# Where the tiles of a decoder trunk begin in SBUF: 160 and 288 bytes past a multiple of 512, or at it

## The chip, the cores and the metric

The kernel runs on one core of a Trainium2 chip. The metric is the time of one execution on the device, in microseconds (us); lower is better. Three executions of the kernel before took 2289.76, 2294.25 and 2301.1 us; the median is 2294.25 us.

## The reference, cut to what matters

Two decoder layers work on 256 tokens of width 2048, all in float32. Each is a mixer with an input and an output projection, and then a dense SwiGLU feed-forward part of width 5632.

```
h = x
for layer in range(2):
    p = rms_norm(h, norm[layer]) @ w_in[layer]
    # layer 0: a gated convolution and RWKV-7;  layer 1: a pooling mixer and latent attention
    h = h + mixer(p) @ w_out[layer]
    xf = rms_norm(h, ffn_norm[layer])
    h = h + (silu(xf @ w_gate[layer]) * (xf @ w_up[layer])) @ w_down[layer]
return rms_norm(h, final_norm)
```

All but a small part of the arithmetic is in the dense products `@ w`.

## The kernel before, in words

**A float32 product from three passes.** Each activation x and each weight w is split into a rounded float32r part (hi) and the rest (lo). A product is then xh·wh + xl·wh + xh·wl, so each 128 rows of the contraction cost three matmuls. A matmul has a stationary operand of 128 columns, which a weight load (PEld in the profile) brings into TensorE, and a moving operand of 256 or 512 columns, which is streamed past it. Every matmul of the dense products changes the stationary operand, so there is one weight load for each matmul, and the load for the next one runs while the present one streams.

**Two forms of the dense product.** `gemm_wt` (L160) takes 128 columns of weights (`wh`, `wl`) as stationary and 256 tokens of `xh` or `xl` as moving: the input projections. `gemm_tok` (L173) takes 128 tokens of `xh` or `xl` as stationary and 512 columns of weights as moving: the output projections and the gate and up products. The down products use `gemm_tok` with `hh` and `hl`, the split hidden activations, as stationary; the keys, queries and values of the odd layer use `lh` and `ll`, the split latents.

**The weights' path.** SP issues a DMA for each half block (`load_next`, L67: `w`, 1024 columns, 512 KB). ScalarE rounds 512 columns of it to `wh` (L96) and VectorE subtracts to give `wl` (L97); `quarter` (L106) hands them to the matmuls. There are 4 buffers of `w` and 6 each of `wh` and `wl`. The instructions' order on each engine is the order of the program's text; nothing is reordered later.

**Where tiles lie.** `build` (L286) opens pools one behind the other, and a pool's tiles lie in the order in which their tags are first asked for. The constants are first, from byte 16,512 of each partition: `ident`, `ones`, `pkt`, `mhalf`, `cos`, `sin` and `h`, which ends at byte 37,024. The pool `xs` follows: `xh` and `xl` (4 buffers of 4096 bytes each), then `dg` (2 x 512 bytes), `ssq` and `rstd` (2 x 32 each), which are asked for later. Then comes the pool `wp`: `w`, `wh`, `wl`; and then the pools of the stages. All buffers of the tags in the table are a multiple of 2048 bytes long, and slices of 128 columns are 512 bytes, so what a tile's start leaves over a multiple of 512 also holds for each operand sliced from it:

| operand | start of the first buffer | over a multiple of 512 |
|---|---|---|
| `xh`, `xl` | 37,024 | 160 |
| `w` | 70,944 | 288 |
| `wh`, `wl` | 87,328 | 288 |
| `hh`, `hl` (feed-forward stages) | 120,096 | 288 |
| `lh`, `ll` (odd layer's latents) | 117,088 | 352 |

Of the kernel before, what the change touches and what calls it, by code (L numbers as in the profile page):

```python
# [10 lines left out]
F32 = mybir.dt.float32  # L11
# [7 lines left out]
P = 128  # L19
T = 256  # L20
# [31 lines left out]
class Trunk:  # L52
# [12 lines left out]

# [1 line left out]
    def load_next(self):  # L67
        """the next half of a block; its split into parts frees the space of the fourth after it"""
        if not self.blocks:
            return  # L70
        src = self.blocks[0]
        w = self.wp.tile([P, 1024], F32, tag="w", name="w", bufs=WBUFS)
        o = self.half * 1024
        if isinstance(src, list):
            for i in range(2):
                self.nc.sync.dma_start(
                    out=w[:, i * 512 : i * 512 + 512], in_=src[2 * self.half + i]
                )
            end = self.half
        else:  # L80
            self.nc.sync.dma_start(out=w, in_=src[:, o : o + 1024])
            end = o + 1024 == src.shape[-1]
        self.loaded.append((w, 0))
        self.half = 0 if end else 1
        if end:
            self.blocks.pop(0)
# [19 lines left out]
    def quarter(self):  # L106
        """the next 512 columns of weights; what waits in the background moves on"""
        self.fill()
        self.tick()
        return self.pend.pop(0)  # L110

# [1 line left out]
    def later(self, n, fn):  # L113
# [22 lines left out]
    def drain(self, gen=None):  # L136
        """emits the background's steps up to the end of gen"""
        while self.lane and (gen is None or any(g is gen for g in self.lane)):
            self.step()
# [6 lines left out]
    def split(self, dst, src, scale=None):  # L146
        """dst (hi, lo) float32r <- src [* scale per partition]"""
        nc = self.nc
        hi, lo = dst
        if scale is None:  # L150
            nc.scalar.activation(hi, src, AF.Copy)  # L151
            nc.vector.tensor_tensor(out=lo, in0=src, in1=hi.bitcast(F32), op=ALU.subtract)  # L152
        else:
            nc.scalar.activation(hi, src, AF.Copy, scale=scale)
            nc.vector.scalar_tensor_tensor(
                out=lo, in0=src, scalar=scale, in1=hi.bitcast(F32),
                op0=ALU.mult, op1=ALU.subtract,
            )

    def gemm_wt(self, X, n=4, tag="mm"):  # L160
        """[128 columns of W, tok] = W^T X over n quarters of 4 k tiles"""
        out = self.ps(tag)[:, :T]
# [10 lines left out]
    def gemm_tok(self, X, kcs, out=None, stop=True):  # L173
        """out [tok, 512] x 2 halves (+)= X W over the k tiles 4 kc .. 4 kc + 3 of each kc"""
        new = out is None
# [13 lines left out]

# [1 line left out]
    def transpose_nb(self, X, gname, nb):  # L191
        """512 columns of h (token-major) -> x^T parts, with the norm's gain folded in"""
        nc = self.nc
# [38 lines left out]
    def finish(self, ps, nb, ssq, X, gname):  # L232
        """adds a layer's last part to 512 columns of h and turns them into x^T parts"""
        self.add_h(ps, nb, ssq)
        self.later(3, lambda: self.transpose_nb(X, gname, nb))

    def out_proj(self, M, n0, before, gname):
        """h += M W: all but the last blocks ahead of the last heads; before(kc) makes M[kc]"""
        pool = self.xs
# [11 lines left out]
        X = self.xtiles()  # L251
# [4 lines left out]

# [1 line left out]
    def order(self):  # L258
# [27 lines left out]
    def build(self):  # L286
# [4 lines left out]
        with (  # L291
# [11 lines left out]
            self.sin = cp.tile([P, T], F32, name="sin")  # L303
            self.h = cp.tile([P, 2, D], F32, name="h")
            nc.vector.memset(self.mhalf, -0.5)
            nc.vector.memset(self.ones, 1.0)
# [14 lines left out]
    def last(self, HX, kcs, ssq):  # L321
        """the last 512 columns and the final norm, one half of the tokens ahead of the other"""
        nc, a, V = self.nc, self.a, self.nc.vector
# [49 lines left out]
    def sums_tok(self, out, xs, w):  # L373
        """out [tok, ...] = sum of x^T w for both halves of the tokens; x [128, 256]"""
        n = w.shape[-1]
# [7 lines left out]
    def rsqrt(self, out, ps, scale, eps):  # L383
        """out = (scale ps + eps) ** -0.5"""
        n = out.shape[-1]
# [5 lines left out]
    def row_bcast(self, rb, rs):  # L391
        """rb [128, 256] <- rs [tok, 2], each token's value on every partition"""
        nc = self.nc
# [6 lines left out]

# [1 line left out]
    def ffn(self, X, ssq, gname, between=None):  # L402
# [60 lines left out]

# [1 line left out]
    def even_mix(self):  # L465
# [6 lines left out]

        # x^T parts, by pieces that alternate with the first weights
        X = self.xtiles()
# [9 lines left out]
        gmask, blk, smask = cst[:, 0:128], cst[:, 128:256], cst[:, 256:516]  # L484
        # 1/rms, as a row on every partition
        rb = tp.tile([P, T], F32, name="rb0")
# [19 lines left out]

        # space of h until x is loaded there
        hv0, hv1 = self.h[:, 0], self.h[:, 1]
# [41 lines left out]
        def first_tiles():  # L550
            """four column tiles at once, so that x^T is wanted no faster than it comes"""
            warm = self.ps()
# [59 lines left out]
        def spread(out, v):  # L612
            """out [128, tok] <- v [tok, (half, head)], each head on its 64 partitions"""
            vx = ta("vx").rearrange("p (t h n) -> p t h n", t=2, h=2)
# [12 lines left out]
        def open_group(grp):  # L627
            """even heads on partitions 0-63 with rows (B | K), odd heads on 64-127 with (K | B)"""
            g = {}
# [12 lines left out]
        def prep_a(ti):  # L642
            """decays and key norms of two heads"""
            i = ti % 4
# [33 lines left out]
            S.activation(ch(Ei), cum[:, :, 1:65], AF.Exp, scale=KAPPA)  # L678
            # 1 / norm of the keys, [tok, half, head]
            kn = tp.tile([P, 4], F32, tag="kn", name="kn", bufs=2)  # L680
# [7 lines left out]
        def prep_b(ti):  # L688
            """keys, values and the Gram matrices of two heads"""
            grp, i = ti // 4, ti % 4  # L690
# [6 lines left out]
            for w in range(4):  # L697
                nc.tensor.transpose(  # L698
                    pv[:, w * P : w * P + P], v[:, w * 64 : w * 64 + P], self.ident
                )  # L700
            # window w has chunk w on rows 0-63 and chunk w + 1 on 64-127
            pvv = pv.rearrange("p (w h n) -> p w h n", w=4, h=2)
# [41 lines left out]
            S.activation(BKt[:, i], pb.rearrange("p (c n) -> p c n", c=4), AF.Copy)  # L744
            # Gram matrices, rows at s, columns (Z | R) at t
            for hh in range(2):
# [11 lines left out]
                )  # L758
                # N goes to TT, its 32 x 32 diagonal blocks also to DG; its place in G takes Z
                for q in range(2):  # L760
# [12 lines left out]
        def recur(grp):  # L773
            """the recurrence over four chunks of 64 tokens, eight heads at a time"""
            g = groups[grp]
            g2, G, TT, UV, BKt, bv = (g[n] for n in ("g2", "G", "TT", "UV", "BKt", "bv"))
            pend, ZRs = g["pend"], g["ZR"]
            nc.sync.dma_start(out=g2, in_=a["g2"][grp])
            # inverse of I - N on 32 x 32 diagonal blocks, one on each partition
            dN = self.dp.tile([16, P, 32], F32, tag="dN", name="dN")  # L780
# [67 lines left out]
            for c in range(4):  # L848
# [44 lines left out]
                yield GAPS['h3']  # L893
            # group norm, bonus, gate
            ycs, sqs = [], []
# [42 lines left out]

        # dense products with the recurrence's steps in their background
        first_tiles()  # L940
# [40 lines left out]

# [1 line left out]
    def rope_tables(self):  # L983
# [85 lines left out]

# [1 line left out]
    def odd_mix(self, X, rs):  # L1071
# [9 lines left out]

        # latents: gain folded into the parts, 1/rms row kept for after the products
        lat, rows = [], []
# [48 lines left out]

        # pooling mixer's input
        up = tp.tile([P, 4, 16 + T], F32, name="up")
# [4 lines left out]

        # keys, values, queries  # L1140
        kn = tp.tile([P, HEADS, T], F32, name="kn")
# [114 lines left out]
        def slots(b, gap):  # L1256
            """heads in turn, each a step behind the one before it"""
            for h in range(4 * b, 4 * b + (4 if b < 2 else 6)):
# [40 lines left out]
def _wt(w):  # L1299
    """[K, N] -> [N/128, 128, (K/128) * 128]: one stationary column tile to a row block"""  # L1300
    K, N = w.shape
# [3 lines left out]
def _tok(w):  # L1305
    """[K, N] -> [N/512, K/512, 128, 4 * 512]"""
    K, N = w.shape
# [125 lines left out]
```

## Time and profile before

| | |
|---|---|
| median of three executions | 2294.25 us |
| span of the profiled execution, first to last instruction | 2288.4 us |
| TensorE matmuls, busy | 2273.3 us (99%), 12,422 |
| TensorE weight loads, busy | 1919.0 us (84%), 12,422 |
| VectorE, busy | 1371.6 us (60%) |
| ScalarE, busy | 1167.5 us (51%) |
| DMA, moved | 405.46 MB, 177 GB/s in the mean |

The span is the profile's own time for its execution; it gives no other, and it is 5.9 us under the median of the three. [...] What counts is the distance from one start to the next, which is read from a piece of the chain of work (its length divided by its matmuls) or from the timeline's start times.

### The profile page before, as it was taken

How to read it: one execution, taken by the hardware profiler on the slowest of the kernel's cores; microseconds unless marked ns; L12 is line 12 of the kernel's file. 1: busy time of each engine (PE TensorE's matmuls, PEld its weight loads, DVE VectorE, ACT ScalarE, POOL GpSimd, SP SyncE). 2: the span in 40 equal slices, each digit the busy share in tenths (PEclk: the TensorE clock that was granted, in tenths of full speed). 3: DMA queues.
4: the chain of work that ended last, by engine and by line, in shares of the span. 5: the costliest groups of instructions: out<-in, count | busy, mean ns of one | idle time of the engine just before them, and what ended most of it. 6: DMA issues, size and time to landing. Idle time of an engine off the chain costs nothing.

```text
span 2288.4 us, 33957 instructions
## 1 busy us (share of the span) xinstructions
PE 2273.3 (99%) x12422; PEld 1919.0 (84%) x12422; DVE 1371.6 (60%) x2432; ACT 1167.5 (51%) x2085; POOL 27.2 (1%) x41
## 2 busy tenths in 40 slices
PE   9999999999999999999999999999999999999998
PEld 9999898778888888888888998788888888888886
DVE  7785587558555555555555677665555555555554
ACT  7655464455454444444455545465444444454454
POOL 0000000000000000000000000000000000000000
PEclk9999999999999999999999999999999999999999
DMA  8455236535555555555555553355555555555554
GB/s 302 134 178 166 93 121 194 170 108 182 184 187 187 184 195 193 185 184 185 187 187 186 185 169 126 126 180 197 186 185 184 184 193 193 185 187 187 181 191 155
DMA packets 124680, 405.46 MB, mean 177 GB/s; under 512 B 24896, under 2 KB 25152, under 8 KB 124128
## 3 DMA queue, kind: packets, MB, share of 16 engines
q1 hardware_dynamic: 122896, 398.31, 52.1%
q0 software_dynamic: 896, 3.80, 0.6%
q8 instruction: 97, 1.59, 0.3%
q10 hardware_dynamic: 720, 1.18, 0.1%
q14 instruction: 71, 0.58, 0.1%
HBM read 400.10 MB, written 3.15 MB: 176 GB/s over the span
## 4 chain that ended last, share of the span: by engine, by line
PE 97%; DVE 1%; DMA 1%; ACT 0%; issue 0%; POOLq 0%; POOL 0%; SPq 0%; DVEq 0%
PE mm L57 88%; PE sm L57 7%; PE sm L434 1%; DVE wl L97 1%; PE sm L198 0%; DMA Nb<-dN 0%; DMA dN<-DG 0%; DVE Tb L806 0%; DVE ou L802 0%; PE sm L1239 0%; ACT wh L96 0%; DMA pkt<-pk 0%; PE sm L698 0%; PE sm L741 0%; DVE h L602 0%
## 5 line engine op out<-in xcount | busy, mean ns | idle before, releaser
L97 DVE TENSOR_TENSOR wl<-w,wh 128x512 fp32r<-128x512 f32 x1482 | 1017.3, 691 | 792.5 <-ACT wh L96 774.8
L96 ACT ACTIVATE wh<-w 128x512 fp32r<-128x512 f32 x1482 | 932.4, 631 | 975.7 <-PE mm L57 696.6
L57 PE MATMUL mm<-wh,xh 128*128 128x512 f32 x1664 | 664.4, 399 | 2.2 <-ACT xh L151 2.2
L57 PE MATMUL mm<-wh,xl 128*128 128x512 f32 x1664 | 656.4, 394 | 1.2 <-DVE xl L152 1.2
L57 PE MATMUL mm<-wl,xh 128*128 128x512 f32 x1664 | 523.1, 395 | 0.0
L57 PEld LDWEIGHTS mm<-wh,xh 128*128 128x128 f32 x1664 | 313.7, 189 | 78.3 <-ACT xh L151 2.7
L57 PEld LDWEIGHTS mm<-wl,xh 128*128 128x128 f32 x1664 | 313.2, 188 | 73.7
L57 PEld LDWEIGHTS mm<-wh,xl 128*128 128x128 f32 x1664 | 313.7, 189 | 71.6 <-DVE xl L152 1.5
L57 PE MATMUL mm<-xh,wh 128*128 128x256 f32 x992 | 286.8, 289 | 1.2 <-ACT wh L96 1.2
L57 PE MATMUL mm<-xh,wl 128*128 128x256 f32 x992 | 280.7, 283 | 0.0
L57 PE MATMUL mm<-xl,wh 128*128 128x256 f32 x992 | 280.6, 283 | 0.0
L57 PE MATMUL mm<-wh,hh 128*128 128x512 f32 x704 | 274.5, 390 | 0.0
L57 PE MATMUL mm<-wh,hl 128*128 128x512 f32 x704 | 273.9, 389 | 0.0
L57 PE MATMUL mm<-wl,hh 128*128 128x512 f32 x704 | 220.1, 389 | 0.0
L57 PEld LDWEIGHTS mm<-xh,wh 128*128 128x128 f32 x992 | 187.9, 189 | 4.5 <-ACT wh L96 1.5
L57 PEld LDWEIGHTS mm<-xl,wh 128*128 128x128 f32 x992 | 188.1, 190 | 0.5
L57 PEld LDWEIGHTS mm<-xh,wl 128*128 128x128 f32 x992 | 187.7, 189 | 0.3 <-DVE wl L97 0.2
L57 PEld LDWEIGHTS mm<-wl,hh 128*128 128x128 f32 x704 | 132.1, 188 | 27.5
L57 PEld LDWEIGHTS mm<-wh,hl 128*128 128x128 f32 x704 | 132.2, 188 | 27.3
L57 PEld LDWEIGHTS mm<-wh,hh 128*128 128x128 f32 x704 | 132.1, 188 | 27.2
L228 DVE TENSOR_TENSOR h<-mm,h 128x512 f32<-128x512 f32 x54 | 34.9, 685 | 4.8 <-PE mm L57 4.7
L57 PE MATMUL mm<-lh,wh 128*128 128x256 f32 x120 | 35.4, 295 | 0.0
(256 smaller groups left out, 1278.0 us busy)
## 6 DMA issues: line engine op xcount, KB each, us to landing
w<-f_gate SPq DMA_DIRECT2D x176, 512.0 KB, 3.7
w<-f_up SPq DMA_DIRECT2D x176, 512.0 KB, 3.6
w<-f_down SPq DMA_DIRECT2D x176, 512.0 KB, 3.6
w<-e_in SPq DMA_DIRECT2D x94, 512.0 KB, 3.9
w<-e_out SPq DMA_DIRECT2D x32, 512.0 KB, 3.7
w<-o_out SPq DMA_DIRECT2D x32, 512.0 KB, 3.6
w<-o_in SPq DMA_DIRECT2D x26, 512.0 KB, 3.6
w<-e_in SPq DMA_DIRECT2D x16, 256.0 KB, 6.1
```

What stands on the lines that cost most here:

```text
L57: return self.nc.tensor.matmul(out, lhsT, rhs, start=start, stop=stop)
L96: nc.scalar.activation(hi, w[:, sl], AF.Copy)
L97: nc.vector.tensor_tensor(out=lo, in0=w[:, sl], in1=hi.bitcast(F32), op=ALU.subtract)
L228: nc.vector.tensor_tensor(out=hs, in0=ps[t], in1=hs, op=ALU.add)
L434: nc.tensor.transpose(pt[:, i * T + t * P : i * T + t * P + P], ac[t][:, (j + i) * P : (j + i + 1) * P], self.ident,)
```

## The change

Two things are added to `build`, ahead of the first instruction, and nothing else acts: the diff otherwise takes out comments and texts that describe functions, and later lines carry numbers that are 3 higher.

```diff
             self.h = cp.tile([P, 2, D], F32, name="h")
+            cp.tile([P, 56], F32, name="gap")
+            for tag, shape in (("dg", [P, P]), ("ssq", [P, 2, 4]), ("rstd", [P, 2])):
+                self.xs.tile(shape, F32, tag=tag, name=tag, bufs=2)
             nc.vector.memset(self.mhalf, -0.5)
```

The tile `gap`, 224 bytes, is never written or read; it moves all that lies behind the constants up by 224 bytes. The loop asks for one tile each of `dg`, `ssq` and `rstd` ahead of time, so that these tags (1152 bytes in all) lie ahead of `xh` instead of behind `xl`. These tiles are not written either. The list of instructions of each engine is the same as before, with the same waits and the same signals; only the addresses of the operands differ:

| operand | over a multiple of 512: before | after |
|---|---|---|
| `ident`, `ones`, `pkt`, `h` (constants) | 128, 128, 128, 160 | the same |
| `xh`, `xl` | 160 | 0 |
| `w`, `wh`, `wl` | 288 | 0 |
| `hh`, `hl` | 288 | 0 |
| `lh`, `ll` | 352 | 64 |
| `dg` | 160 | 384 |
| other tiles of the stages' pools | a | a + 224 (mod 512) |

Between two tiles that both lie behind `xl` the distance is what it was; between `xh` or `xl` and any tile behind them, and between the constants and everything else, it is not.

## Rows read from the trace of the kernel before

**Rows 1.** Page, part 1: engine, busy us, share of the span, instructions.
```profile
PE 2273.3 (99%) x12422; PEld 1919.0 (84%) x12422; DVE 1371.6 (60%) x2432; ACT 1167.5 (51%) x2085; POOL 27.2 (1%) x41
```
**Rows 2.** Page, part 4: the chain that ended last, by engine and by line.
```profile
PE 97%; DVE 1%; DMA 1%; ACT 0%; issue 0%; POOLq 0%; POOL 0%; SPq 0%; DVEq 0%
PE mm L57 88%; PE sm L57 7%; PE sm L434 1%; DVE wl L97 1%; PE sm L198 0%; DMA Nb<-dN 0%; DMA dN<-DG 0%; DVE Tb L806 0%; DVE ou L802 0%; PE sm L1239 0%; ACT wh L96 0%; DMA pkt<-pk 0%; PE sm L698 0%; PE sm L741 0%; DVE h L602 0%
```
**Rows 3.** Groups of matmuls: out<-operands, shape, xcount | busy us, mean ns | idle before.
```profile
L57 PE MATMUL mm<-wh,xh 128*128 128x512 f32 x1664 | 664.4, 399 | 2.2 <-ACT xh L151 2.2
...
L57 PE MATMUL mm<-xh,wh 128*128 128x256 f32 x992 | 286.8, 289 | 1.2 <-ACT wh L96 1.2
...
L57 PE MATMUL mm<-wh,hh 128*128 128x512 f32 x704 | 274.5, 390 | 0.0
...
L57 PE MATMUL mm<-lh,wh 128*128 128x256 f32 x120 | 35.4, 295 | 0.0
...
L57 PE MATMUL sm<-xh,wl 128*128 128x256 f32 x32 | 9.1, 284 | 0.0
```
**Rows 4.** Chain in order of time, feed-forward stages: start us, us, what, matmuls.
```profile
797.83 175.27 PE mm L57 x768
...
1156.24 27.22 PE mm L57 x120
1184.33 27.22 PE mm L57 x120
...
1587.39 44.79 PE mm L57 x192
1633.06 44.62 PE mm L57 x192
```
**Rows 5.** Timeline of PE in a gate product: start us, us, operation.
```profile
1700.77 0.40 PE L57 MATMUL mm<-wh,xh 128*128 128x512 f32 x1
1701.01 0.39 PE L57 MATMUL mm<-wh,xl 128*128 128x512 f32 x1
1701.24 0.40 PE L57 MATMUL mm<-wh,xh 128*128 128x512 f32 x1
1701.48 0.39 PE L57 MATMUL mm<-wh,xl 128*128 128x512 f32 x1
```
**Rows 6.** Timeline of PE in a down product.
```profile
1836.94 0.39 PE L57 MATMUL mm<-wh,hh 128*128 128x512 f32 x1
1837.17 0.39 PE L57 MATMUL mm<-wh,hl 128*128 128x512 f32 x1
1837.39 0.39 PE L57 MATMUL mm<-wh,hh 128*128 128x512 f32 x1
```
**Rows 7.** Windows 1690:1724 and 1824:1858: PE, PEld, DVE, ACT, POOL, clock, DMA, GB/s.
```profile
1690.00:1724.00 34.00, 34.00 (x152) 27.43 (x151) 18.25 (x27) 16.42 (x27) 0.00 (x0) 1.00 0.54 182
1824.00:1858.00 34.00, 34.00 (x151) 28.15 (x150) 18.44 (x28) 15.80 (x25) 0.00 (x0) 1.00 0.57 187
```
**Rows 8.** Timeline of PE in the odd layer's values: latents stationary, weights moving.
```profile
1388.84 0.40 PE L57 MATMUL mm<-wh,lh 128*128 128x512 f32 x1
...
1390.70 0.63 PE L57 MATMUL mm<-wl,lh 128*128 128x512 f32 x2
```
**Rows 9.** Chain in order of time, even layer's input projection (256 columns).
```profile
129.83 71.20 PE mm L57 x600
...
319.47 4.38 PE mm L57 x36
```
**Rows 10.** Chain in order of time, odd layer's keys and queries (256 columns).
```profile
1360.08 9.89 PE mm L57 x84
```
**Rows 11.** Groups of VectorE and ScalarE that make the weights' parts.
```profile
L97 DVE TENSOR_TENSOR wl<-w,wh 128x512 fp32r<-128x512 f32 x1482 | 1017.3, 691 | 792.5 <-ACT wh L96 774.8
L96 ACT ACTIVATE wh<-w 128x512 fp32r<-128x512 f32 x1482 | 932.4, 631 | 975.7 <-PE mm L57 696.6
```
**Rows 12.** Waits: who waited for whom, us in total, times, longest.
```profile
ACT wh L96 <- DMA w<-e_in: 7.4, 7, 2.0
```
**Rows 13.** Chain in order of time, window 340:400: the recurrence's way through HBM.
```profile
349.19 6.58 DMA dN<-DG
...
356.34 8.08 DMA Nb<-dN
```
**Rows 14.** DMA issues: out<-in, queue, count, KB each, median us to landing.
```profile
TD<-dT SPq DMA_DIRECT2D x2, 256.0 KB, 3.5
```
**Rows 15.** Window 388.9:392.4, columns as in rows 7: TensorE at half clock.
```profile
388.90:392.40 3.50, 3.20 (x8) 2.53 (x9) 3.50 (x11) 3.50 (x11) 0.00 (x0) 0.51 0.10 36
```

## The prediction

> **What bounds the kernel now.** The first view to read is the busy time by engine: TensorE is busy 99% of the span and VectorE 60% [rows 1]. The chain of work that ended last is the second, and it says that this is no accident of pipelining: 97% of it lies on TensorE, 88% of the span on the dense products' matmuls, while the makers of the weights' parts have 1% or less [rows 2]. So only what changes the distance from one matmul to the next changes the time by much. The third view, the groups of matmuls, gives the counts and shows that they hardly ever wait for a producer (2.2 us in 1664 of them) [rows 3]. The fourth, the chain in order of time, gives the distances, since a piece without a wait is its length divided by its matmuls:
>
> In a gate or up product (`xh`, `xl` stationary, weights moving, 512 columns) 192 matmuls take 44.62 us, 232.4 ns each; another piece of 192 takes 44.79 us, 233.3 ns. In a down product (`hh`, `hl` stationary, the same moving operand) 120 take 27.22 us, 226.8 ns each. The long piece of 768 is 576 of the second kind and 192 of the first: 130.6 + 44.6 = 175.2 us, as it stands there [rows 4].
>
> The two kinds have the same shape, the same number of weight loads and the same clock. The reader is to see in the timeline that they differ in their beat: the down product's starts are 0.23 and 0.22 us apart, the gate product's 0.24, 0.23, 0.24 us [rows 5, 6]. [...] What differs is where the stationary operand begins: `hh` and `wh` both lie 288 bytes over a multiple of 512, `xh` lies at 160 against 288. A third pair bears this out: in the odd layer's values the stationary `lh` lies at 352 and the moving weights at 288, and 8 matmuls take 1390.70 - 1388.84 = 1.86 us, 232.5 ns each [rows 8]. I read from it that a weight load and the stream beside it disturb each other by an amount that depends on the distance of their starts, and that a distance of 0 modulo 512 is the better case of the three.
>
> **The change part by part.** No instruction is added, removed or moved; each engine has the same list with the same waits. What is left are pairs of addresses.
>
> First, `xh` and `xl` as stationary against `wh` and `wl`. The distance goes from 128 to 0, which is that of the down product. There are 3 x 1664 = 4992 such matmuls [rows 3]. At 226.8 instead of 232.4 ns each saves 5.6 ns, in all **28.0 us**, nearly all of it on the chain. [...]
>
> Second, the input projections, where `xh` and `xl` are moving, 256 columns: 3 x 992 + 3 x 32 = 3072 matmuls [rows 3]. They stand at 71.20 / 600 = 118.7 ns [rows 9], with a distance of 128 between the starts. No row shows a distance of 0 with 256 columns. The nearest row has the same shape and a distance of 64: the keys and queries, 9.89 / 84 = 117.7 ns [rows 10]. On the good side, if 256 columns fell in the proportion of 512 (226.8 / 232.4), they would stand at 115.8 ns and save 8.9 us. On the bad side, the slowest piece of this form, 4.38 / 36 = 121.7 ns [rows 9], would cost 3.0 ns each, 9.2 us. I take the nearest row: 1.0 ns each, **3.1 us** saved.
>
> Third, pairs whose distance stays: `hh` against `wh` (0) and `lh` against `wh` (64). All of them move up by 224 bytes; I cost that at 0, since only the distance has been seen to matter. If the absolute start mattered too, the third case below prices it.
>
> Fourth, the small matmuls. The chain has about 8% of the span on them (7% and 1% in rows 2), some 183 us. Many join two tiles of one pool, whose distance stays; those with `ident`, `ones` or `h` get another. If all of them moved by the 2.4% that separates the two beats, it would be 4.4 us either way. I take 0.
>
> Fifth, VectorE, ScalarE and DMA with new addresses. VectorE stood idle 792.5 us before the operations that make `wl`, ScalarE 975.7 us before those that make `wh` [rows 11]: even 10% more on each of 1482 x 691 ns (102 us) would be hidden by six matmuls, 1.39 us, for each pair of them. Where that cover is gone, around 335 to 389 us when VectorE is on the chain, 10% of some 50 us would cost 5 us; 0 is taken. The weights' DMAs are not on the chain, and ScalarE waited for them 7.4 us in all in the first layer [rows 12]. Only the recurrence's way through HBM stands on the chain, 6.58 and 8.08 us [rows 13]; if each fell to the 3.5 us of the third transfer of that kind [rows 14], it would save 7.7 us, and if each took 8% more (3.6 to 3.9 us is what like transfers of the weights differ by), it would cost 1.2 us. I take 0. [...]
>
> The sum: 28.0 + 3.1 = 31.1 us off the traced span of 2288.4 us, 2257.3 us. The span lies 5.9 us under the median of the runs shown, so the same saving against that median gives 2294.25 - 31.1 = **2263 us**. What is late next is again TensorE: at 226.8 ns, six matmuls are 1.36 us, still about twice the 0.69 us that VectorE needs for its share.
>
> **The rivals.** *No effect.* The beats in rows 4 differ for a reason other than the starts, for instance something in the accumulation of gate and up. For it: only three pairs of starts are seen at 512 columns. Against it: equal load in rows 7, and the values (rows 8), which are neither gate nor up and share the slow beat. Then nothing is saved and the time is 2294 us. [...]
>
> *More than the distance.* A start at a multiple of 512 may also take away what is left between two matmuls. From rows 4 and 10, 256 more columns cost 226.8 - 117.7 = 109.1 ns, so 512 columns are 218.2 ns and 8.6 ns is a fixed part. If half of it went (4.3 ns), the saving would be 4992 x 9.9 + 3072 x 5.3 = 65.7 us, and 4.3 ns on each of the 3 x 704 + 3 x 120 = 2472 matmuls with `hh` and `lh`, 10.6 us: 76.3 us in all, 2218 us. If all of it went, 2172 us. Against it: every row has a fixed part, whatever its starts. [...]
>
> *Slower.* Two streams that begin at equal places could ask the same part of SBUF at each step and be held up at each: the slow half of the gate product's beat, 0.24 us [rows 5], would become the rule. 4992 x (240 - 232.4) ns is 37.9 us more, 2332 us. It decides for slower as soon as the matmuls with `xh` stationary stand over 233 ns. Against it: the down product has equal remainders already, and the better beat.
>
> **How the numbers follow.** The forecast has 0.71, more than the distance 0.13, no effect 0.10, slower 0.06. Within the forecast the second term reaches from -9.2 to +8.9 us, so the saving is 18.8 to 36.9 us; with the scatter of the runs shown (4.5 us below and 6.9 above the median) that is 2253 to 2282 us. Of the others I take in the upper part of the second case and the gains bounded above, which gives 2232 to 2283 us. About 0.5% (11.5 us) is what a measurement here can tell from no change. Faster by more: the forecast and the second case, 0.84, less 0.02 for the edges of the forecast's range, 0.82. Within it: 0.10 and half of that edge, 0.11. Slower: 0.06 and the other half, 0.07.
>
> **What would show it.** A piece of 192 gate matmuls at 192 x 226.8 ns = 43.5 us, with starts 0.22 to 0.23 us apart, shows the first term right; 44.6 us shows it wrong. The down product's 120 at 27.22 us and the keys' 84 at 9.89 us should stay; if they shrink, the absolute start matters. A long piece of the even layer's input projection, 600 at about 70.6 us, tests the second term. The prediction is wrong if the gate product keeps two steps in its beat, or if the recurrence's transfers change.

## The result, and the profile after

The changed kernel takes 2267.91 us (median of four, 2266.38 to 2272.67) against 2292.01 us before (median of four, 2289.2 to 2301.1): the ratio is 0.989 with a 95% interval of 0.9868 to 0.9911. The medians are 24.1 us apart, the interval lies below 1, and the time lies in the stated range. The forecast of 2263 us had named 31.1 us.

The page of the changed kernel shows the same engines in the same order; part 1 (busy us, share, instructions) and the first line of part 4 (the chain that ended last) answer to [rows 1, 2]:

```profile
PE 2256.8 (99%) x12422; PEld 1925.3 (85%) x12422; DVE 1371.7 (60%) x2432; ACT 1166.7 (51%) x2085; POOL 27.1 (1%) x41
```

```profile
PE 96%; DVE 2%; DMA 1%; ACT 1%; issue 0%; POOLq 0%; POOL 0%; SPq 0%; DVEq 0%; ACTq 0%
```

The chain in order of time (start us, us, what, matmuls) holds the pieces on which the prediction rested. They answer to [rows 9], [rows 4] and, from a window on the odd layer, [rows 10]:

```profile
131.20 72.00 PE mm L57 x600
...
799.34 174.10 PE mm L57 x768
...
1107.56 43.54 PE mm L57 x192
1151.97 27.22 PE mm L57 x120
```

```profile
1356.58 9.89 PE mm L57 x84
```

The reader is to see that a gate piece of 192 went from 44.62 to 43.54 us (226.8 ns a matmul, the beat of the down product), that the down product's 120 and the keys' 84 stayed at 27.22 and 9.89 us to the last digit, and that the input projection's 600 went the other way, from 71.20 to 72.00 us (120.0 ns). The timeline of PE (TensorE) in a gate product, which answers to [rows 5], has lost its two steps: the starts are 0.23, 0.23 and 0.22 us apart.

```profile
1700.43 0.39 PE L57 MATMUL mm<-wh,xl 128*128 128x512 f32 x1
1700.66 0.39 PE L57 MATMUL mm<-wh,xh 128*128 128x512 f32 x1
1700.89 0.39 PE L57 MATMUL mm<-wh,xl 128*128 128x512 f32 x1
1701.11 0.61 PE L57 MATMUL mm<-wl,xh 128*128 128x512 f32 x2
```

With these two beats the sum is 4992 x 5.6 = 28.0 us saved and 3072 x 1.3 = 4.0 us lost, 24.0 us; between the medians it is 24.1 us. The traced spans differ by less, 2288.4 - 2270.9 = 17.5 us, since TensorE ran for 17 us of the first layer's recurrence at a granted clock of 0.50 in the traced execution of the changed kernel, and the trace of before has 1.00 there (last section).

### The profile page after: what moved, and what is told of

The parts are those of the page before. It is cut to its first block, busy times and chain, and to the rows that moved or that the text cites. A ratio compares the mean times of both kernels' runs of the same rounds, so it can differ in the third digit from the quotient of the medians.

```text
span 2270.9 us, 33957 instructions
## 1 busy us (share of the span) xinstructions
PE 2256.8 (99%) x12422; PEld 1925.3 (85%) x12422; DVE 1371.7 (60%) x2432; ACT 1166.7 (51%) x2085; POOL 27.1 (1%) x41
## 4 chain that ended last, share of the span: by engine, by line
PE 96%; DVE 2%; DMA 1%; ACT 1%; issue 0%; POOLq 0%; POOL 0%; SPq 0%; DVEq 0%; ACTq 0%
PE mm L57 88%; PE sm L57 7%; PE sm L437 1%; DVE wl L97 1%; PE sm L198 0%; DMA Nb<-dN 0%; DMA dN<-DG 0%; DVE Tb L809 0%; DVE ou L805 0%; ACT wh L96 0%; PE sm L1242 0%; DMA pkt<-pk 0%; PE sm L701 0%; PE sm L744 0%; DVE h L605 0%
## 5 line engine op out<-in xcount | busy, mean ns | idle before, releaser
L57 PE MATMUL mm<-wh,xh 128*128 128x512 f32 x1664 | 657.2, 395 | 1.0 <-ACT xh L151 1.0
L57 PE MATMUL mm<-wl,xh 128*128 128x512 f32 x1664 | 515.0, 391 | 0.0
```

What stands on the lines that cost most here:

```text
L57: return self.nc.tensor.matmul(out, lhsT, rhs, start=start, stop=stop)
```

## The experiments

Theory D says that what counts is the distance between the start of the stationary operand and that of the moving one. Rival A says that it is the multiples of 512 themselves. Distances are given as the start of `xh` (or `hh`, `lh`) less that of `wh`, so 160 against 288 is -128, which modulo 256 is 128. In runs 2 to 9 the gap is gone; in runs 5, 6, 7 and 9 an unused result (`junk`) also shares a buffer with the recurrence's solver in the even layer.

**1. The gap alone.**

```diff
             cp.tile([P, 56], F32, name="gap")
-            for tag, shape in (("dg", [P, P]), ("ssq", [P, 2, 4]), ("rstd", [P, 2])):
-                self.xs.tile(shape, F32, tag=tag, name=tag, bufs=2)
```

> The 224-byte gap alone: wh, wl, hh, hl begin at multiples of 512, but xh and xl at 384 over one, so the distance from xh to wh is 128 as in the kernel before. Theory D (only the distance of the two starts counts): gate pieces of 192 at 44.6 us (232.4 ns each), input projection 600 in 71.2 us (118.7 ns), down products 226.8 ns; time as before, 2292 us. Rival A (it is the weights' own start at a multiple of 512 that helps): gate pieces at 43.5 us, input projection at 72.0 us, time about 2268 us.

2293.42 us against 2292.64, ratio 1.0003 (0.9986 to 1.0021). The weights lie at multiples of 512 here, and the beats are those of before. The chain in order of time of this run:

```profile
130.48 71.20 PE mm L57 x600
...
528.86 44.62 PE mm L57 x192
...
1160.73 27.22 PE mm L57 x120
```

The weights' own alignment brings nothing that these executions can tell (the interval is 0.2% either way).

**2. The early tiles alone.**

```diff
-            cp.tile([P, 56], F32, name="gap")
             for tag, shape in (("dg", [P, P]), ("ssq", [P, 2, 4]), ("rstd", [P, 2])):
```

> The three early tiles alone: xh, xl, wh, wl, hh, hl all begin 288 bytes over a multiple of 512, so every distance is that of the changed kernel while nothing lies at a multiple of 512. Theory D: gate pieces 43.5 us, input projection 600 in 72.0 us, time as the changed kernel, about 2268 us. Rival A (the multiples of 512 count): gate pieces 44.6 us, input projection 71.2 us, about 2292 us.

2267.13 us, ratio 0.9886 (0.9859 to 0.9912): the whole effect of the change, with x, the weights and the hidden activations 288 bytes over a multiple of 512. The same view:

```profile
131.18 72.00 PE mm L57 x600
...
534.41 43.54 PE mm L57 x192
...
1153.52 27.22 PE mm L57 x120
```

So the 224-byte gap does nothing that can be told; moving `xh` and `xl` to a distance of 0 from `wh` does it all, the gain and the loss.

**3 and 4. Other distances.** Early tiles, no gap, and unused tiles ahead of `w` and ahead of the feed-forward stages' and the odd layer's tiles (here those of run 3; run 4 has 480 bytes, 256, 32 and 448).

```diff
-            cp.tile([P, 56], F32, name="gap")
...
+            self.wp.tile([P, 112], F32, tag="padw", name="padw", bufs=1)       # 448 bytes
...
             with tc.tile_pool(name="ff0", bufs=1) as self.tp:
+                self.tp.tile([P, 8], F32, tag="pad", name="pad")               # 32 bytes
...
             with tc.tile_pool(name="odd", bufs=1) as self.tp:
+                self.tp.tile([P, 16], F32, tag="pad", name="pad")              # 64 bytes
...
             with tc.tile_pool(name="ff1", bufs=1) as self.tp:
+                self.tp.tile([P, 120], F32, tag="pad", name="pad")             # 480 bytes
```

> Early tiles, and an unused tile ahead of w, so that xh lies 64 past wh (mod 512); in the first feed-forward stage hh lies 32 past wh, in the second 32 before it; the latents lie 128 past wh. Theory D: xh as stationary takes the latents' beat of before, 232 to 234 ns; xh as moving takes the keys' 117.7 ns (600 in 70.6 us); the down products leave 226.8 ns, in the first stage or in both. Rival: the keys' 117.7 ns comes from their short groups of 12 matmuls, and the input projection stays between 118.7 and 120.0 ns; rival A: the down products stay at 226.8 ns whatever their distance, since that is a property of the down product.

2315.85 us in one execution. The chain in order of time: the input projection (distance 64), a gate piece (64), a down piece of the first stage (32), the odd layer's keys (128) and the second stage's piece of 576 down and 192 up products (-32 and 64):

```profile
128.82 70.66 PE mm L57 x600
...
534.07 44.79 PE mm L57 x192
...
1170.81 28.00 PE mm L57 x120
...
1377.22 9.97 PE mm L57 x84
...
1833.61 179.20 PE mm L57 x768
```

The down product leaves its 226.8 ns for 233.3 (28.00 / 120), so that beat was no property of the down product. The second stage's 576 stand at (179.20 - 44.8) / 576 = 233.3 ns as well. The input projection takes 117.8 ns (70.66 / 600), the keys' beat of before, and the keys, now at 128, take 118.7 ns (9.97 / 84), the input projection's beat of before. Theory D holds here, rival A falls.

This run also ends a rival that was not named: that the stationary operand's place disturbs TensorE through what ScalarE and VectorE read and write beside it. At the kernel's end TensorE still works on the down product while these two and the DMA queues stand still. The window (columns as in [rows 7]), first of this run and then of the kernel before, and the first and last start of PE in the window of this run:

```profile
2298.40:2302.00 3.60, 3.60 (x17) 2.91 (x16) 0.00 (x0) 0.00 (x0) 0.00 (x0) 1.00 0.00 0
2272.90:2276.40 3.50, 3.50 (x17) 2.92 (x16) 0.00 (x0) 0.00 (x0) 0.00 (x0) 1.00 0.00 0
```

```profile
2298.40 0.40 PE L57 MATMUL mm<-wh,hh 128*128 128x512 f32 x1
...
2301.90 0.39 PE L57 MATMUL mm<-wh,hh 128*128 128x512 f32 x1
```

15 steps in 3.50 us are 233.3 ns, as before it, with the two others idle. In the kernel before, at a distance of 0, the 15 steps from 2272.87 to 2276.27 us are 226.7 ns each.

> As the run before with other distances: xh 32 past wh, hh 256 past wh in the first feed-forward stage and 64 before it in the second, latents 96 past wh. Theory D with a period of 512: the first down product leaves 226.8 ns at 256, the second too (at -64). With a period of 256: the first stays at 226.8 ns. No row tells what 32 gives for xh: between 226.8 and 233 ns at 512 columns, 117.7 to 120.0 ns at 256.

2295.82 us in one execution. The input projection (distance 32), a gate piece (32), a down piece of the first stage (256), and the second stage's piece of 768 (down -64, up 32):

```profile
129.79 70.67 PE mm L57 x600
...
525.48 44.80 PE mm L57 x192
...
1158.40 27.22 PE mm L57 x120
...
1818.13 176.71 PE mm L57 x768
```

A distance of 256 is as good as 0 (27.22 us for 120), so if the beat with 512 columns repeats with the distance, its period is 256 or a divisor of it; 128 and 64 are none, since they give other beats than 0 (232.4 ns in run 1, 233.3 in run 3). At -64 the 576 down products take (176.71 - 44.8) / 576 = 229.0 ns: between the two.

**5. Twenty-two distances in one kernel.** The tiles of `hh`, `hl`, `xh` and `xl` are 256 bytes longer. The slices of `hh` and `hl` begin at an offset of their own in each block (`HOFFS`, in elements of 4 bytes), those of the input projections' x at one for each four of the 16 k tiles.

```diff
-                hh = self.tp.tile([P, 4, T], F32R, tag="hh", name="hh", bufs=6)
-                hl = self.tp.tile([P, 4, T], F32R, tag="hl", name="hl", bufs=6)
+                o = HOFFS[b if gname else NFB + b]
+                hh = self.tp.tile([P, 4 * T + 64], F32R, tag="hh", name="hh", bufs=6)
+                hl = self.tp.tile([P, 4 * T + 64], F32R, tag="hl", name="hl", bufs=6)
+                hh, hl = (
+                    v[:, o : o + 4 * T].rearrange("p (a t) -> p a t", a=4) for v in (hh, hl)
+                )
```

> The layout with every distance at 0 modulo 256, but hh and hl begin at a distance of their own in each of the 22 blocks of hidden activations (0, 4, 8, 16, 24, 32, 40, 48, 56, 64, 80, 96, 112, 128, 144, 160, 176, 192, 208, 224, 240, 252 bytes past wh), and x in the input projections at 32, 16, 48, 224 (even layer, one distance for each 4 of the 16 k tiles) and 8, 40, 192, 160 (odd layer). Theory D: the beat with 512 columns is a function of the distance modulo 256: 226.8 ns at 0, 233.3 at 32 and 64, 234 at 96, 232.3 at 128, 228.9 at 192, 233.3 at 224, as in the runs before, whichever block has it. Rival: the beat belongs to the block or the stage, and a distance met in another block gives another beat by more than 1 ns. With 256 columns: 117.0 ns at 32; the rest unknown between 115 and 120 ns. A beat below 226.8 ns at some distance would show that part of what is left between two matmuls can be had.

2277.4 us in one execution. The timeline of PE at the starts of three blocks of 24 matmuls of one down product, at distances 4, 8 and 16, and of the block behind them:

```profile
797.58 0.39 PE L59 MATMUL mm<-wh,hh 128*128 128x512 f32 x1
...
803.16 0.39 PE L59 MATMUL mm<-wh,hh 128*128 128x512 f32 x1
...
808.69 0.40 PE L59 MATMUL mm<-wh,hh 128*128 128x512 f32 x1
...
814.29 0.40 PE L59 MATMUL mm<-wh,hh 128*128 128x512 f32 x1
```

5.58, 5.53 and 5.60 us for 24: 232.5, 230.4 and 233.3 ns at 4, 8 and 16 bytes. Worked out in the same way from the start times of this run, the mean steps in ns by distance, each within its own block (the nine distances left out lie between 229.8 and 233.4; 240 and 252 without the last product, of which more below):

| columns | distance: mean step |
|---|---|
| 512 | 0: 226.9; 4: 232.4; 8: 230.7; 16: 233.3; 32: 233.0; 64: 233.5; 96: 234.1; 128: 233.5; 160: 233.2; 192: 229.0; 224: 233.1; 240: 228.0; 252: 226.7 |
| 256 | 8: 120.0; 16: 117.5; 32: 117.3; 48: 118.1; 64: 117.8; 160: 117.3; 192: 114.7; 224: 118.0 |

With 512 columns nothing is better than 0, and a shift of 4 bytes upwards already loses 5.5 ns. All but one of the values expected from the runs before came within 1 ns (128: 233.5 against 232.3). With 256 columns 0 (120.0 ns in run 2) is among the worst, and 192 the best.

A shift of 4 bytes downwards (252) loses nothing in three of its four down products, but in the last one, whose matmuls come in another order and after the makers of the weights' parts have finished, it does. The timeline of PE, 18 steps at 252 in the second of the four and in the last:

```profile
2206.21 0.39 PE L59 MATMUL mm<-wh,hh 128*128 128x512 f32 x1
...
2210.29 0.39 PE L59 MATMUL mm<-wh,hh 128*128 128x512 f32 x1
```

```profile
2261.38 0.40 PE L59 MATMUL mm<-wh,hh 128*128 128x512 f32 x1
...
2265.56 0.40 PE L59 MATMUL mm<-wh,hh 128*128 128x512 f32 x1
```

4.08 us are 226.7 ns a step, 4.18 us are 232.2. The same distance can thus have two beats, and theory D does not hold to the letter. What decides between the two was not tried.

**6. Both distances.** The input projections' x begins 32 bytes further in its buffers; x as the stationary operand and the hidden activations stay at 0, the latents at 64, as in the changed kernel.

```diff
-    def xtiles(self):
-        xh = [self.xs.tile([P, 4, T], F32R, tag="xh", name="xh") for _ in range(4)]
+    def xtiles(self, offs=(0, 0, 0, 0)):
+        xh = [self.xs.tile([P, 4 * T + 64], F32R, tag="xh", name="xh") for _ in range(4)]
...
-        X = self.xtiles()
+        X = self.xtiles((8, 8, 8, 8))
```

> Each use gets the distance that suits it: x of the two input projections begins 32 bytes past wh (modulo 256), all else at a distance of 0. The tiles of xh and xl are 256 bytes longer for that, and the unused result of the sums of squares shares a buffer with the recurrence's solver in the even layer. Theory D: 4992 matmuls stay at 226.8 ns and 3072 go from 120.0 to about 117.1 ns, 8.9 us less than the changed kernel, about 2259 us. Rival (what 256 columns gain is lost to the first stage's other waits): 2264 to 2268 us.

2260.83 us, ratio to the kernel before 0.9864 (0.9842 to 0.9885). The chain in order of time:

```profile
128.58 70.00 PE mm L57 x600
...
520.46 43.54 PE mm L57 x192
```

Both beats are had at once: 116.7 ns with 256 columns in the input projection and 226.8 with 512. The gain over the changed kernel is 7.1 us between medians taken at different times, where 8.9 was expected.

**7. Both distances, with 192.** As 6 with `xtiles((48, 48, 48, 48))`, and 128 bytes ahead of the odd layer's tiles, which puts the latents at 192 too.

> As the run with both distances, but x of the input projections and the latents begin 192 bytes past wh (modulo 256) instead of 32 and 64. In the run with many distances the 256-column matmuls at 192 stood at 114.7 ns, those at 32 at 117.3 ns. Theory D: 3072 matmuls go from 117.0 to 113 to 115 ns, 7 us less, 360 of the latents from 117.8 as well, 1 us: about 2253 us. Rival (114.7 ns was an effect of the neighbours, since only 140 of them stood at 192 between other distances): 117 to 118 ns and 2260 us.

2256.29 us (2253.28 to 2262.11), ratio 0.9839 (0.9809 to 0.9868): the best of the kernels, 36.6 us under the kernel before. The even layer's input projection stands at 68.01 / 600 = 113.4 ns in this piece, and 114.6 is the mean of all steps of both input projections; the neighbours had not made the 114.7 ns of run 5.

```profile
127.51 68.01 PE mm L57 x600
...
521.44 43.54 PE mm L57 x192
...
1255.15 20.63 PE mm L57 x180
...
1280.84 19.79 PE mm L57 x168
...
1343.02 9.89 PE mm L57 x84
```

Two parts of the expectation were missed. The odd layer's input projection, at the same 192, has a piece at 114.6 ns (20.63 / 180) and one at 117.8 (19.79 / 168), and the keys' 84, now at 192, stay at 9.89 us, where 113 to 115 ns had been expected for them too. The time is 3.3 us over the expected 2253 us. So at 192 as well one distance has more than one beat.

**8. Which pair disturbs which.** `xh` at a distance of 0, `xl` at 64.

```diff
         xh = [self.xs.tile([P, 4, T], F32R, tag="xh", name="xh") for _ in range(4)]
+        if self.first:
+            self.xs.tile([P, 16], F32, tag="padx", name="padx", bufs=1)
+            self.first = False
         xl = [self.xs.tile([P, 4, T], F32R, tag="xl", name="xl") for _ in range(4)]
...
-            cp.tile([P, 56], F32, name="gap")
...
+            self.wp.tile([P, 48], F32, tag="padw", name="padw", bufs=1)
+            self.first = True
```

The 64 bytes ahead of `xl` and the 192 ahead of `w` put `xh` 256 bytes from `wh`, which is 0 modulo 256.

> xh at a distance of 0 from wh, xl at 64, all else at 0 as in the changed kernel. In a gate product the stationary parts follow each other as xh, xl, xh, xl, xh, xh, all with the same moving block at the start of wh or wl. Theory L (the load of the next stationary part and the present stream disturb each other): the steps that begin with xh and load xl are long (two of six), those that begin with xl and load xh are 226.8 ns or less. Theory S (what counts is the stationary part already in place against its own stream): the steps that begin with xl are the long ones. Rival (both or neither): all six steps change, as with all parts at 64, 233 ns each.

Inconclusive. 2281.4 us in one execution; the gate pieces lie between 43.54 and 44.8:

```profile
1018.18 43.97 PE mm L57 x192
...
1107.88 44.47 PE mm L57 x192
```

From the start times, steps from `xh` that load `xl` take 229.9 ns in the mean, steps from `xl` that load `xh` 230.3 (before a product with `wl`) and 233.4 (before one with `wh`), steps between two `xh` 228.5. Each kind is sometimes 226 to 227 and sometimes 230 to 238 ns. Neither theory L nor S is borne out, nor the rival, by which all would stand at 233. Why the steps don't tell the pairs apart was not shown. The question stays open.

**9. Around the good distances.** As 5, with x at 176 to 216 and `hh` at other values.

> As the run with many distances, with others: x of the input projections at 184, 192, 200, 208 (even layer) and 176, 188, 196, 216 (odd layer) bytes past wh, hh in 22 blocks at 252, 248, 244, 236, 232, 228, 220, 216, 212, 204, 200, 196, 188, 184, 180, 172, 12, 20, 28, 36, 44, 52. Theory D: 192 gives again 113 to 115 ns with 256 columns, and 252 again 226.6 to 228 ns with 512. If what counts is a grid of 64 bytes, 184 and 200 stand clearly over 192 (by 1 ns or more); if the beat is smooth in the distance, they stand within 1 ns of it. With 512 columns no distance is expected under 226.6 ns.

2281.3 us in one execution. The timeline of PE in the even layer, at the starts of three groups of 12 matmuls at distances 184, 192 and 200, and of the group behind them:

```profile
151.34 0.28 PE L59 MATMUL mm<-xh,wh 128*128 128x256 f32 x1
...
152.78 0.28 PE L59 MATMUL mm<-xh,wh 128*128 128x256 f32 x1
...
154.16 0.28 PE L59 MATMUL mm<-xh,wh 128*128 128x256 f32 x1
...
155.60 0.28 PE L59 MATMUL mm<-xh,wh 128*128 128x256 f32 x1
```

1.44, 1.38 and 1.44 us for 12: 120.0, 115.0 and 120.0 ns. In the mean of the run's steps 188 gives 119.0 and 196 gives 121.6 ns, so 192 is a sharp place and no broad valley. With 512 columns the good place is as narrow, from 252 (227.3 here) to 0: 248 and 244 have 233.3 and 233.2 ns, 4 had 232.4 in run 5, and 12 has 233.5. No 512-column distance came under 226.6 ns.

## Why the prediction was right, and where it was off

**What bounds the kernel** was read rightly: the beat of the dense products. The two runs with one part each show that the beat depends on the distance of the starts (44.62 us at -128 in run 1, 43.54 at 0 in run 2, the same instructions in both). That it does not hang on the load of the other engines was to be read from [rows 7], where both kinds have like loads and a clock of 1.00, and is shown by the end of run 3, where the slow beat goes on with the others idle.

**First term, 4992 matmuls with `xh` and `xl` stationary.** Forecast 28.0 us, measured 44.62 to 43.54 us for 192, so 5.6 ns each and 28.0 us. This is the step that made the forecast right, and it came from reading two products of the same shape against each other in the trace of before. That the distance is all that counts was too strong: runs 5 and 7 have two beats at one distance (226.7 and 232.2 ns at 252, 114.6 and 117.8 at 192), though no second one was seen at 0 with 512 columns. That the starts move the beat is also measured on the down product: with nothing changed but where the operands start, its step goes from 226.8 to 233.3 ns (runs 2 and 3).

**Second term, 3072 matmuls with `xh` and `xl` moving.** This is the term that was mis-sized. The forecast took the nearest row, a distance of 64, for a distance of 0 that no row showed: 117.7 ns, 3.1 us saved. Measured were 120.0 ns and 4.0 us lost, inside the bounds of -9.2 to +8.9 us. The distance of 0, which is best with 512 columns, is among the worst with 256. The difference, 7.1 us, is what separates the forecast's 31.1 us from the measured 24.1 us; that the time still lies in the range is owed to the bounds set for this term, not to its value. The fault in the step was to take "near" by shape, when the runs show that 4 bytes can matter: a beat at one distance says little on another.

**Third term, pairs whose distance stays.** Taken at 0, and they stayed: 27.22 us for the down product's 120 and 9.89 us for the keys' 84, although all these tiles moved by 224 bytes. That also ends the rival *more than the distance*.

**Fourth and fifth terms.** The small matmuls were taken at 0. The transposes with `ident`, whose distance to their partner changes by 224 bytes, take 0.87 us for 8 on the chain of before and on that of the changed kernel:

```profile
706.04 0.87 PE sm L434 x8
```

```profile
709.64 0.87 PE sm L437 x8
```

The makers of the weights' parts took 691 and 631 ns an operation before and after. The recurrence's transfers on the chain took 6.84 and 7.12 us, where [rows 13] has 6.58 and 8.08: 0.7 us less in all. On the chains of runs 1, 2, 6, 7 and 9 the first takes 6.53 to 7.00 us and the second 7.28 to 9.78, so one trace can't tell this from scatter, and the sign of being wrong that the prediction named for them did not show.

```profile
351.72 6.84 DMA dN<-DG
...
359.12 7.12 DMA Nb<-dN
```

**The other rivals.** *No effect* falls with runs 1 to 3, which move the beat by where the operands start and by nothing else. *Slower* was the wrong way round for 512 columns, and right in kind for 256: equal starts are a bad case there. It stayed small because those are 3072 matmuls with a loss of 1.3 ns against 4992 with a gain of 5.6.

## What to carry to other kernels

Where TensorE is bound by a stream of matmuls that each load a new stationary operand, compare the beats of products of the same shape; if they differ under the same load, look at where the two operands begin, here modulo 256 bytes (256 gave the 226.8 ns of 0 in run 4), before looking at the schedule. The distance that suits depends on the form: here 0 for 512 moving columns (226.8 ns) and 192 for 256 (113.4 ns at best, in run 7), and a start at a multiple of 512 was worth nothing by itself: run 1 has it for the weights without a gain, run 2 the whole gain without it. A few bytes of padding reach it, but each form must be measured, since places 4 bytes apart can differ by 5 ns a matmul (226.9 and 232.4 ns at 0 and 4 in run 5), and one distance can have two beats in two products (226.7 and 232.2 ns at 252 there).

## What the runs showed of the hardware that was not expected

**The beat hangs sharply on the distance, and not on it alone.** With 512 columns it takes 226.8 ns at 0, 229.0 at 192 and mostly 230 to 237 elsewhere in these runs (252 and 240 excepted); with 256 columns 113 to 118 ns at 192 against 117 to 122 elsewhere. Why 256 is as good as 0, and what chooses where one distance has two beats, was not shown.

**The clock falls in the recurrence, in some executions.** The changed kernel's trace has TensorE's granted clock at 0.50 from 452.7 to 459.5 us and twice more, in 466.4 to 473.2 and 480.0 to 483.3 us; the trace of before has such a stretch elsewhere, at 0.51 [rows 15]. The window (PE, PEld, DVE, ACT, POOL, clock, DMA, GB/s) shows 33 matmuls, where the same stretch before, at a clock of 1.00, shows 69:

```profile
452.70:459.50 6.80, 6.80 (x33) 4.97 (x34) 2.25 (x5) 1.42 (x3) 0.00 (x0) 0.50 0.00 0
```

```profile
452.70:459.50 6.80, 6.80 (x69) 4.89 (x70) 3.50 (x8) 3.02 (x6) 0.00 (x0) 1.00 0.15 46
```

TensorE had been busy throughout in both (12.8 of 12.8 us in the changed kernel and 16.0 of 16.0 in the one before, up to 452.6 us); in the 13 us ahead of it its work was 64-column matmuls between the dense ones (116 of the first and 24 of the second from 440 to 452.6 us in the changed kernel, 112 and 23 before). Matmul for matmul, the changed kernel's trace falls back by 5.7 us from 440 to 473 us and by 7.2 us up to 505 us. That covers what the traced span lacks against the medians, 24.1 - 17.5 = 6.6 us. The kernel before has executions with a lower clock too: beside run 7 its mean granted clock went from 0.998 to 0.992 and its span from 2288.1 to 2298.6 us with it; where in these executions the clock fell is not known. In run 1, at the distances of before, the mean granted clock is 0.992 to 0.998 in ten executions, in the changed kernel 0.993 to 0.996 in four. Whether the new addresses make such falls more frequent was not tried.
